# Eleven of layer 1's weight tiles split during layer 0's output product, and the parts of layer 1's weights kept in DRAM and reloaded by GpSimd's queue

## The chip, the core and the metric

The kernel runs on one core of a Trainium2 chip. A core has TensorE (PE, with its weight loads PEld), VectorE (DVE), ScalarE (ACT), GpSimd (POOL) and SyncE (SP), which share an on-chip memory; DMAs bring data from DRAM and back. Each engine works through its own list of instructions in order; a DMA is issued from the list of SP, ACT or POOL and stands in that engine's DMA queue. The metric is the time of one execution in microseconds on the device.

## The reference

Two layers on a residual stream of 1024 tokens by 1024 features, in float32. Layer 0 is a gated pooling mixer, layer 1 a gated sliding-window attention that reads one shared K/V. Cut to what matters:

```python
for l in range(2):
    shift, scale, gate = split(silu(c) @ ada_w[l] + ada_b[l], 3)
    if l == 0:
        h = rmsnorm(x, norm_g[0]) * (1 + scale) + shift
        u, z = split(h @ w_in, 2)
        p = pools(u) - u
        y = (group_matmul(p, w_group) * a_scale * silu(z)) @ w_out
    else:
        k, v = blocks((rmsnorm(x, kv_norm_g) * (1 + kvscale) + kvshift) @ w_kv)
        h = rmsnorm(x, norm_g[1]) * (1 + scale) + shift
        q, z = split(h @ b_w_in, 2)
        o = softmax_with_sinks(q * 64 ** -0.5 @ k + bias) @ v
        y = (o * silu(z)) @ b_w_out
    x = x + gate * y
return rmsnorm(x, final_g)
```

## The kernel before

Tokens lie along the free dimension, features on the 128 partitions. A float32 product is made of three matmuls: every operand is split into a rounded high part (ACT casts it) and the rest (DVE or POOL subtracts the high part), and high·high, high·low and low·high are added up in PSUM. A weight tile is 128 x 1024, 512 KB. `load_w` (line 133) fetches one on SP's queue into one of two `raw` buffers and splits it with `split_w` (line 119) into one of two pairs `wh`, `wl`.

The stages, in time: the pooling mixer's projections and pools (up to 424 us of the span); layer 0's output product (424 to 565); its last pieces, woven with the first norm of layer 1 (565 to 609); layer 1.

**Layer 0's output product** (lines 835 to 864) runs over `order`, 16 steps (n, half): output feature block n, half of the inner dimension. A step is 48 matmuls for n below `LATE` = 5 (both halves of the tokens, `q`), 24 after that. When the second half of an n is done, DVE adds it to `x` (`residual`), ACT squares and DVE sums the squares. The weights of step i+1 are fetched and split ahead of step i. `gather` brings back the gate products that the mixer kept in DRAM, `again_x` reloads `x`. Beside them `ada_step` (line 249) does the rest of the modulation: one of 48 tiles of `ada_rest` is loaded by SP into one of three `tmp` buffers, and DVE makes the dot product with `silu(c)` (`ada_dot`, line 239 in the profile). 18 of the 48 are done in the mixer, 30 here, with the table `ADA` of 16 numbers, one for each step. Here PE's order is written; the other engines' is left to the scheduler.

**Layer 1** (lines 1338 to 1376) runs over `specs`, for the first half of the tokens (q = 0) and then the second (q = 1): for each of four pairs of head rows two query tiles and two gate tiles of `wb` (`project`), between them the two tiles of `wkv` (`keys`, `values`), and output tiles of `wbo` (`project_out`, `out_quarter`). So most tiles are loaded and split twice, once for each half of the tokens. `load_w` for the next tile is called ahead of each product. `load_last` (line 1218) does the four `wbo` tiles of the second part with the subtraction on POOL. Beside the products the attention of block after block is woven in: `attend` has DVE and ACT make the scores and the softmax into `pt` (lines 1107 to 1119), PE transposes them (L1125), ACT and DVE split the result (`cur`, L1128 and L1129), POOL masks it (`prev`, `cur`, L1134 and L1137), PE multiplies with V (L1148). POOL also copies a column into each `pt` (L1093) and makes the low parts of modulated tiles (L167). PE's order is written here too, by a clock of estimated costs; the other engines' is the scheduler's.

## Time and profile before

| | us |
|---|---|
| median of three runs | 986.33 (985.83 to 986.64) |
| the profiled execution | 984.87 |
| its span, first to last instruction | 982.6 |
| PE busy in the span | 961.9 |
| the last chain, 962.6 to 982.6: statistics, POOL's multiplications (6.33), output | 20 |

In a window row the columns are: stretch, its length, then busy time (number of instructions) of PE, PEld, DVE, ACT and POOL, granted clock, share of the DMA engines and GB/s. In a row of a group: line, engine, operation, output and inputs, shapes, number, then busy time, mean ns of one, and idle time ahead of them with what ended it. A row of waits has the total, the number and the longest. A timeline row has start, duration, engine, line. A row of a DMA queue has packets, MB and the share of 16 engines; a row of DMA issues has the number, the size and the median time from issue to landing.

### The profile page before, as it was taken

The page shows a single profiled execution, that of the slowest core. Times are in us where ns is not written, and L with a number is a line of the kernel's source. Part 1 is how long each engine was busy: PE and PEld are TensorE (multiplying, and loading weights), DVE is VectorE, ACT ScalarE, POOL GpSimd, SP SyncE. Part 2 cuts the span into 40 slices and gives each one's busy share as a digit, 9 for nine tenths or more (in the row PEclk, how much of TensorE's full clock was granted, in tenths as well). Part 3 has the DMA queues.
Part 4 walks back from the last instruction along what each step waited for, and adds up shares of the span by engine and source line. Part 5 has one row for each costly group of instructions (what it writes and reads, how often), then busy time and mean ns, then how long its engine had stood idle before and what let it go on. Part 6 is the DMA issues. An engine that isn't in the chain of part 4 may idle for free.

```text
span 982.6 us, 12696 instructions
## 1 busy us (share of the span) xinstructions
PE 961.9 (98%) x4538; PEld 801.2 (82%) x4538; DVE 775.7 (79%) x1411; ACT 458.1 (47%) x902; POOL 145.0 (15%) x173
## 2 busy tenths in 40 slices
PE   8999999999999999999999999999999999999996
PEld 6788888888888887888888888877888888887786
DVE  5897978677978699676782278599899878889985
ACT  6534434333433244551111145486677546566544
POOL 2100000000000000000000000052324313335723
PEclk9999999999999999999999999999999999999998
DMA  9453622264225411779861223222211221223222
GB/s 331 183 174 114 192 103 65 78 201 150 65 85 194 150 64 57 262 267 327 305 216 65 86 64 130 86 65 69 82 66 64 87 86 65 64 88 106 86 87 86
DMA packets 40625, 125.67 MB, mean 128 GB/s; under 512 B 4465, under 2 KB 6641, under 8 KB 40434
## 3 DMA queue, kind: packets, MB, share of 16 engines
q1 hardware_dynamic: 40416, 123.82, 37.6%
q10 hardware_dynamic: 146, 1.05, 0.3%
q8 instruction: 35, 0.57, 0.2%
q14 instruction: 28, 0.23, 0.1%
HBM read 111.22 MB, written 13.63 MB: 127 GB/s over the span
## 4 chain that ended last, share of the span: by engine, by line
PE 78%; DVE 16%; issue 2%; ACT 2%; POOL 1%; DMA 0%; POOLq 0%; DVEq 0%; SPq 0%; ACTq 0%
PE ps_d L214 14%; PE ps_S L214 9%; PE ps_d L636 9%; PE ps_d L203 6%; PE ps_d L204 6%; PE ps_d L205 6%; PE ps_S L636 4%; PE ps_o L214 4%; PE ps_tp L214 3%; DVE wl L123 2%; PE ps_d L374 2%; PE ps_o L636 2%; PE ps_tp L636 2%; DVE tmp L542 2%; PE ps_tp L1125 1%
## 5 line engine op out<-in xcount | busy, mean ns | idle before, releaser
L121 ACT CAST wh<-raw 128x1024 fp32r<-128x1024 f32 x73 | 76.5, 1048 | 101.4 <-PE ps_d L214 78.5
L123 DVE TENSOR_TENSOR wl<-raw,wh 128x1024 fp32r<-128x1024 f32 x73 | 94.2, 1290 | 26.7 <-ACT wh L121 22.8
L203 PE MATMUL ps_d<-hm,wh 128*128 128x512 f32 x288 | 113.8, 395 | 0.0
L205 PE MATMUL ps_d<-hm,wl 128*128 128x512 f32 x288 | 112.4, 390 | 0.3 <-DVE wl L123 0.3
L204 PE MATMUL ps_d<-hm,wh 128*128 128x512 f32 x288 | 112.4, 390 | 0.0
L239 DVE CUSTOM_DVE_ANT_0 tmp<-tmp,cact,pk 128x1024 f32<-128x1024 f32 x48 | 60.7, 1282 | 33.2 <-DMA tmp<-ada_rest 32.9
L214 PE MATMUL ps_d<-gh,wh 128*128 128x512 f32 x224 | 82.0, 389 | 0.0
L214 PE MATMUL ps_S<-gh,wh 128*128 128x512 f32 x192 | 64.5, 390 | 0.0
L205 PEld LDWEIGHTS ps_d<-hm,wl 128*128 128x128 f32 x288 | 54.1, 188 | 12.6 <-DVE wl L123 1.1
L636 PE MATMUL ps_d<-hs,ws 128*128 128x512 f32 x264 | 63.4, 389 | 0.0
L1115 ACT ACTIVATE pt<-pt,nm 128x129 f32<-128x129 f32 x128 | 50.2, 394 | 26.8 <-DVE nm L1111 24.6
L203 PEld LDWEIGHTS ps_d<-hm,wh 128*128 128x128 f32 x288 | 54.1, 188 | 10.2
L204 PEld LDWEIGHTS ps_d<-hm,wh 128*128 128x128 f32 x288 | 54.2, 188 | 10.0
L636 PEld LDWEIGHTS ps_d<-hs,ws 128*128 128x128 f32 x264 | 49.5, 188 | 10.3
L542 DVE TENSOR_TENSOR tmp<-tmp 128x1039 f32<-128x1039 f32 (+3 forms) x40 | 49.4, 1235 | 6.8 <-ACT tmp L672 5.7
L612 ACT CAST ws<-tw 128x512 fp32r<-128x512 f32 x44 | 26.8, 621 | 53.9 <-PE ps_tp L214 15.1
L636 PE MATMUL ps_d<-ha,ws 128*128 128x512 f32 x216 | 51.9, 389 | 0.0
L534 POOL MEMSET tmp<- 128x16 f32 x16 | 1.7, 111 | 331.4 <-DVE tmp L542 115.9
L214 PEld LDWEIGHTS ps_d<-gh,wh 128*128 128x128 f32 x224 | 42.1, 188 | 8.7
L636 PEld LDWEIGHTS ps_d<-ha,ws 128*128 128x128 f32 x216 | 40.5, 188 | 8.4
L147 POOL TENSOR_TENSOR rs<-v,mhalf 128x4 f32<-128x4 f32 (+1 forms) x7 | 8.2, 1164 | 241.6 <-DVE v L145 241.6
L214 PE MATMUL ps_d<-gh,wl 128*128 128x512 f32 x112 | 43.6, 389 | 0.0
(294 smaller groups left out, 2492.0 us busy)
## 6 DMA issues: line engine op xcount, KB each, us to landing
tmp<-ada_rest SPq DMA_DIRECT2D x48, 512.0 KB, 4.7
raw<-wb SPq DMA_DIRECT2D x32, 512.0 KB, 3.3
raw<-wa SPq DMA_DIRECT2D x28, 512.0 KB, 3.7
raw<-wao SPq DMA_DIRECT2D x20, 512.0 KB, 4.1
ad<-ada_first SPq DMA_DIRECT2D x16, 512.0 KB, 5.0
x<-xT SPq DMA_DIRECT2D x32, 256.0 KB, 5.9
raw<-wbo SPq DMA_DIRECT2D x16, 512.0 KB, 3.3
kept_g<-tmp SPq DMA_DIRECT2D x14, 512.0 KB, 2.9
```

What stands on the lines that cost most here:

```text
L121: nc.scalar.copy(out=wh, in_=raw)
L123: nc.vector.tensor_sub(out=wl, in0=raw, in1=wh.bitcast(F32))
L203: mm(ps, lh, acts(k, 0), start=k == 0, stop=False)
L204: mm(ps, lh, acts(k, 1), start=False, stop=False)
L205: mm(ps, ll, acts(k, 0), start=False, stop=k == n - 1)
L214: mm(p, lhs, acts(k, hl, q), start=start and k == 0 and s == 0, stop=stop and k == n - 1 and s == 2)
L239: nc.vector.tensor_tensor_reduce(out=raw, in0=raw, in1=ca, scale=0.5, scalar=pk[:, bcol:bcol + 1], op0=ALU.mult, op1=ALU.add, accum_out=ad ...
L374: mm(psu[i, q], w0[k // 2][:, k % 2, w, i * P:(i + 1) * P], block(k, q)[hl], start=k == 0 and s == 0, stop=k == KT - 1 and s == 2)
L542: nc.vector.tensor_add(out=nx[:, 2 * s - 1:], in0=cur[:, 2 * s - 1:], in1=cur[:, s - 1:PAD + T - s])
L612: nc.scalar.copy(out=ws[i][:, 0, :], in_=src)
L636: mm(ps, lhs, acts(k, hl), start=start and k == 0 and s == 0, stop=k == 3 and s == 2, skip_group_check=True)
L1115: nc.scalar.activation(pt[:, i, :P + 1], pt[:, i, :P + 1], AF.Exp, bias=nm[:, i:i + 1], scale=-1.0, accum_out=den[:, i:i + 1])
```

## The change

`ADA` becomes six numbers for the first six steps (24 dots, loaded by SP as before). From step 6 on, the order of all five engines is written: the weights of step i+2 are fetched and those of step i+1 split, and a list `JOBS` of 6 dots (A) and 11 splits of `wb` tiles (S) is worked off, each with its load asked three jobs ahead on POOL's queue. The high part of such a tile goes to one of two `stage` slots, the low part replaces the tile in its `tmp` buffer; both are stored in DRAM by POOL's queue (`keep`). Layer 1 then takes the parts of a tile from DRAM where they are kept (`load_any`, two tiles ahead, three pairs of buffers by `pair_tiles`), on POOL's queue. A tile that isn't kept is loaded by SP, split, and its parts are stored by SP for the second half of the tokens; the parts of `wkv` and of the first query tile, split at the end of layer 0, are stored too. `load_last` goes: its four tiles are loaded by SP and split by ACT and DVE. In the tail two output products of the second half of the tokens come ahead of the four of the first half.

```diff
-ADA = (0, 0, 0, 2, 4, 4, 4, 4, 4, 4, 1, 1, 1, 1, 0, 0)
+ADA = (0, 0, 2, 6, 8, 8)
+BESIDE = 6
+JOBS = ("AAS", "AAS", "SSA", "SSA", "S", "S", "S", "S", "S", "")
...
+    def keep(key, hi, lo, queue=nc.sync):
+        kept_w[key] = [kp.tile([P, 1024], F32, name="kw") for _ in range(2)]
+        for dst, src in zip(kept_w[key], (hi, lo)):
+            queue.dma_start(dst, src.bitcast(F32))
+
+    def pair_tiles():
+        tags = (("raw", "raw"), ("wh", "wl"), ("wh", "wl"))[turns[0] % 3]
+        turns[0] += 1
+        return [wp.tile([P, 1024], F32R, tag=t, name="w2") for t in tags]
...
+            staged = [1, 8, 9, 2, 3, 10, 11, 4, 5, 12, 13]
+            def ask():
+                if not jobs:
+                    return
+                raw = tmp()[:, :1024]
+                kind = jobs.pop(0)
+                if kind == "A":
+                    i = rest_at[0]
+                    nc.gpsimd.dma_start(raw, ada_rest[i])
+                    rest_at[0] += 1
+                    asked.append(lambda: ada_dot(raw, cact, *rest_cols[i]))
+                else:
+                    i = staged.pop(0)
+                    nc.gpsimd.dma_start(raw, wb[i])
+                    asked.append(lambda: stage_split(i, raw))
+            def stage_split(i, raw):
+                hi = stage_hi[i % 2].rearrange("p a c -> p (a c)")
+                nc.scalar.copy(out=hi, in_=raw)
+                lo = raw.bitcast(F32R)
+                nc.vector.tensor_sub(out=lo, in0=raw, in1=hi.bitcast(F32))
+                keep(("b", i), hi, lo, nc.gpsimd)
...
+        with tc.manual_schedule(engines={ET.PE, ET.Activation, ET.DVE, ET.Pool, ET.SP}):
+            stage_hi = [slot("stage") for _ in range(2)]
+            raw = fetch(wao[order[BESIDE + 1]])
+            jobs, asked = list("".join(JOBS)), []
+            for _ in range(3):
+                ask()
+            for i in range(BESIDE, len(order)):
+                if i + 1 < len(order):
+                    ws[order[i + 1]] = split_w(*raw)
+                if i + 2 < len(order):
+                    raw = fetch(wao[order[i + 2]])
+                if i < KT:
+                    again_x(i)
+                for _ in JOBS[i - BESIDE]:
+                    asked.pop(0)()
+                    ask()
+                out_half(i)
...
+            if key in again:
+                keep(again[key], *w)
...
-    def load_last():
-        raw = wp.tile([P, 1024], F32, tag="raw", name="raw")
-        nc.sync.dma_start(raw, wbo[1, len(last_w)])
-        w = hp.tile([P, 2, T], F32R, tag="h", name="wo")
-        nc.scalar.copy(out=w[:, 0, :], in_=raw)
-        nc.gpsimd.tensor_sub(out=w[:, 1, :], in0=raw, in1=w[:, 0, :].bitcast(F32))
-        last_w.append((w[:, 0, :], w[:, 1, :]))
+    def load_any(key):
+        stays = key[0] == "o" and key[1] == 1
+        if stays:
+            t = hp.tile([P, 2, T], F32R, tag="h", name="wo")
+            w = t[:, 0, :], t[:, 1, :]
+            last_w.append(w)
+        else:
+            w = pair_tiles()
+        if key in kept_w:
+            for dst, src in zip(w, kept_w[key]):
+                nc.gpsimd.dma_start(dst, src)
+        else:
+            raw = bp.tile([P, 1024], F32, tag="raw1", name="raw1", bufs=2)
+            nc.sync.dma_start(raw, (wb if key[0] == "b" else wbo)[key[1:]])
+            nc.scalar.copy(out=w[0], in_=raw)
+            nc.vector.tensor_sub(out=w[1], in0=raw, in1=w[0].bitcast(F32))
+            if not stays:
+                keep(key, *w)
+        return w
...
-        *woven(project_out(0, 1) + project_out(1, 0)[:2], (0, 2, 4, 6)),
-        stats(0), project_out(1, 0)[2], finish(0, 4, FINISH[0]),
-        *project_out(1, 0)[3:],
+        *project_out(1, 0)[:2],
+        *project_out(0, 1),
+        project_out(1, 0)[2], stats(0), project_out(1, 0)[3], finish(0, 4, FINISH[0]),
+        project_out(1, 0)[4],
...
-        loaded = {srcs[0]: got["wq"]}
+        loaded = {srcs[0]: got["wq"], srcs[1]: load_any(specs[srcs[1]][0])}
...
-                nxt = srcs.index(i) + 1
+                nxt = srcs.index(i) + 2
                 if nxt < len(srcs):
-                    loaded[srcs[nxt]] = load_w(specs[srcs[nxt]][0])
+                    loaded[srcs[nxt]] = load_any(specs[srcs[nxt]][0])
```

What that does to the order, at three places. First DVE in layer 0's output product, around the end of step 9. Before, the last dot stands ahead of step 7's residuals, and from there on the rows are only weight splits (`wl`), two residuals (L686) and two sums of squares (L195) for each n:

```order
L239 ISA tmp_4271,adac_110<-tmp_4271,cact_119,pk_73 128x1024
L239 ISA adac_110 128x1
L686 SCALAR_TENSOR_TENSOR x_3425<-ps_tp_3856,adac_110,x_3425 128x512
L686 SCALAR_TENSOR_TENSOR x_3425<-ps_d_3857,adac_110,x_3425 128x512
L123 TENSOR_TENSOR wl_3998<-raw_3994,wh_3996 128x1024
L195 TENSOR_TENSOR sqh_3628<-sqh_3628,sq_3988 128x512
L195 TENSOR_TENSOR sqh_3630<-sqh_3630,sq_3991 128x512
L123 TENSOR_TENSOR wl_4066<-raw_4062,wh_4064 128x1024
L686 SCALAR_TENSOR_TENSOR x_3426<-ps_o_4000,adac_110,x_3426 128x512
L686 SCALAR_TENSOR_TENSOR x_3426<-ps_d_4001,adac_110,x_3426 128x512
L123 TENSOR_TENSOR wl_4140<-raw_4136,wh_4138 128x1024
```

The same place in the change, where `wl_4132` is the split for step 10 and `wl_4213` that for step 11 (L880 is `stage_split`, L258 the dot, L705 the residual):

```order
L258 ISA tmp_3997,adac_112<-tmp_3997,cact_121,pk_75 128x1024
L258 ISA adac_112 128x1
L128 TENSOR_TENSOR wl_4132<-raw_4059,wh_4130 128x1024
L880 TENSOR_TENSOR tmp_4067<-tmp_4067,stage_3896 128x1024
L880 TENSOR_TENSOR tmp_4075<-tmp_4075,stage_3895 128x1024
L258 ISA tmp_4078,adac_112<-tmp_4078,cact_121,pk_75 128x1024
L258 ISA adac_112 128x1
L705 SCALAR_TENSOR_TENSOR x_3428<-ps_o_4080,adac_112,x_3428 128x512
L705 SCALAR_TENSOR_TENSOR x_3428<-ps_d_4081,adac_112,x_3428 128x512
L214 TENSOR_TENSOR sqh_3636<-sqh_3636,sq_4205 128x512
L214 TENSOR_TENSOR sqh_3638<-sqh_3638,sq_4208 128x512
L128 TENSOR_TENSOR wl_4213<-raw_4134,wh_4211 128x1024
```

Two tile splits and a dot now stand between the weight split of step 10 and step 9's residuals, and the split for step 11 has moved behind the sums of squares. `tmp_4067` and `tmp_4075` are tiles 3 and 10 of `wb`, `tmp_4078` the last tile of `ada_rest`.

Second, POOL in the same stage. Before, its list has nothing there:

```order
L534 MEMSET tmp_2906 128x16
L534 MEMSET tmp_2925 128x16
L147 TENSOR_TENSOR rs_4367<-v_4365,mhalf_87 128x4
L1093 COPY pt_4811<-nsink_107 128x4
L1093 COPY pt_4889<-nsink_107 128x4
```

In the change 39 DMAs stand between the last memset and `rs`. Twelve of them, with `tmp_3925` tile 8, `tmp_3986` tile 9, `tmp_3989` tile 2, and `kw` the kept parts:

```order
L872 DMA tmp_3925<-wb 128x1024
L872 DMA tmp_3986<-wb 128x1024
L872 DMA tmp_3989<-wb 128x1024
L147 DMA kw_3993<-stage_3895 128x1024
L147 DMA kw_3994<-tmp_3925 128x1024
L867 DMA tmp_3997<-ada_rest 128x1024
L147 DMA kw_4063<-stage_3896 128x1024
L147 DMA kw_4064<-tmp_3986 128x1024
L872 DMA tmp_4067<-wb 128x1024
L147 DMA kw_4071<-stage_3895 128x1024
L147 DMA kw_4072<-tmp_3989 128x1024
L872 DMA tmp_4075<-wb 128x1024
```

The load of `tmp_3997` waits until the store from `tmp_3925` has landed, and the stores of tile 9 stand behind it; the load of `tmp_4067` waits for the dot on `tmp_3997`.

Third, POOL in layer 1, at the second half of the tokens. Before, a copy into `pt` and two masks for each block:

```order
L1134 AFFINE_SELECT prev_6403<-cur_6400 128x1024
L1137 AFFINE_SELECT cur_6400<-cur_6400 128x1024
L1093 COPY pt_6641<-nsink_107 128x4
L1134 AFFINE_SELECT prev_6534<-cur_6531 128x1024
L1137 AFFINE_SELECT cur_6531<-cur_6531 128x1024
L1093 COPY pt_6733<-nsink_107 128x4
```

In the change (L1165 is the copy, L1206 and L1209 the masks, `w2` a kept part on its way back):

```order
L1165 COPY pt_6744<-nsink_109 128x4
L1301 DMA w2_6675<-kw_4146 128x1024
L1206 AFFINE_SELECT prev_6641<-cur_6638 128x1024
L1301 DMA w2_6676<-kw_4147 128x1024
L1209 AFFINE_SELECT cur_6638<-cur_6638 128x1024
L1301 DMA w2_6709<-kw_4219 128x1024
L1301 DMA w2_6710<-kw_4220 128x1024
L1165 COPY pt_6834<-nsink_109 128x4
```

Each load waits until PE has left the buffer that it fills; here one stands ahead of both masks of a block and another between them. In all 66 such loads are in POOL's list.

More of the change, by code (lines that the diff above doesn't have):

```diff
@@ L66, in trunk @@
     pp = ctx.enter_context(tc.tile_pool(name="psum", bufs=1, space=PSUM))
+    kp = ctx.enter_context(tc.tile_pool(name="kept", bufs=1, space=bass.MemoryType.DRAM))
     BANKS = {"d": 4, "S": 2, "tp": 1, "o": 1}
@@ L1025, in keys @@
             return done(ps)
-        return wkv[0], lambda w: gemm_steps(w, 0, hk, KT, done)
+        return ("kv", 0), lambda w: gemm_steps(w, 0, hk, KT, done)
     vts = {}
@@ L1035, in values @@
             return done(ps)
-        return wkv[1], lambda w: gemm_steps(w, 0, hk, KT, done)
+        return ("kv", 1), lambda w: gemm_steps(w, 0, hk, KT, done)
     def values_split(q):
@@ L1177, in run @@
                 yield from gemm_steps(w, i * 512, acts, 4, done)
-        return wbo[part, n2], run
+        return ("o", part, n2), run
     def bare(f):
```

45 lines of the change are left out of this document (21 added, 24 removed).

## The prediction

> **What bounds the kernel now.** I read the page first, then the windows of each stage, then what PE waits for. Times count from the span's start.
>
> ```profile
> span 982.6 us, 12696 instructions
> PE 961.9 (98%) x4538; PEld 801.2 (82%) x4538; DVE 775.7 (79%) x1411; ACT 458.1 (47%) x902; POOL 145.0 (15%) x173
> 424.00:490.00 66.00, 66.00 (x293) 54.66 (x292) 46.12 (x70) 16.93 (x25) 0.00 (x0) 1.00 0.91 314
> 520.00:530.00 10.00, 10.00 (x46) 8.26 (x44) 1.23 (x1) 1.05 (x1) 0.00 (x0) 1.00 0.18 52
> 600.00:950.00 350.00, 342.72 (x1713) 286.85 (x1712) 304.83 (x712) 216.33 (x508) 125.19 (x118) 1.00 0.26 84
> 650.00:670.00 20.00, 16.75 (x85) 13.74 (x84) 19.68 (x45) 17.02 (x38) 13.28 (x12) 1.00 0.22 74
> PE ps_tp L1125 <- DVE pt L1119: 6.1, 5, 1.6
> PE ps_tp L154 <- POOL rs L147: 1.1, 1, 1.1
> ```
>
> PE sets the time, and its number of matmuls does not change. Only its idle time can move. In the window rows the number behind the length is PE's busy time: the two rows of layer 0's output product (424 to 565) have none idle, layer 1 from 600 to 950 has 350 − 342.72 = 7.3 us idle. 3.25 of these lie in 650 to 670, where DVE works 19.68 of 20 us. 6.1 us, in five waits, are waits of the softmax transposes for DVE's last multiplication. So the change can win at most about 7 us here, and can lose in layer 0 as well, where DMA is busy at a share of 0.91 until 490 and nearly idle later.
>
> **What layer 1 loses in work.**
>
> ```profile
> L123 DVE TENSOR_TENSOR wl<-raw,wh 128x1024 fp32r<-128x1024 f32 x45 | 60.0, 1334 | 12.2 <-ACT wh L121 9.9 <-PE ps_o L1149 1.7
> L121 ACT CAST wh<-raw 128x1024 fp32r<-128x1024 f32 x45 | 47.0, 1045 | 15.2 <-issue 7.6 <-PE ps_d L204 6.4 <-ACT qt L1062 0.9
> L1224 POOL TENSOR_TENSOR wo<-raw,wo 128x1024 fp32r<-128x1024 f32 x4 | 10.6, 2652 | 4.3 <-ACT wo L1223 4.2
> ```
>
> These rows are of 600 to 983. Layer 1 splits 49 tiles now: 45 casts on ACT with 45 subtractions on DVE, and 4 more with the subtraction on POOL. Afterwards 12 are left (4 of `wb`, 8 of `wbo`), all on ACT and DVE. DVE is relieved of 33 × 1.334 = 44 us, ACT of 37 × 1.045 = 39 us, POOL of 10.6 us. POOL gets 66 loads of parts. In 650 to 670 DVE had 45/350 × 20 = 2.6 splits, 3.4 us; with 16.3 of 20 us its queue no longer stays full, and the matmuls that waited for `pt` find it ready. I take all five waits away (6.1 us) and give back 0.4 for masks that come behind loads on POOL (below): **−5.7 us**. The bounds: −7.3 (everything idle) and −3 (half the waits stay, because ACT's part of the same chain becomes the late one).
>
> **Is a kept tile there in time?** The three pairs of buffers are used in turn. A pair comes free when PE ends the tile before the current one, and is needed two tiles on. A tile is 24 matmuls; at 342.72/1713 = 0.2 us each two tiles are 9.6 us, more with the attention between them.
>
> ```profile
> raw<-wao SPq DMA_DIRECT2D x7, 512.0 KB, 3.2
> q1 hardware_dynamic: 6346, 20.98, 87.5%
> tmp<-ada_rest SPq DMA_DIRECT2D x29, 512.0 KB, 4.9
> kept_g<-tmp SPq DMA_DIRECT2D x13, 512.0 KB, 2.9
> 438.78 0.33 SPq L130 DMA_DIRECT2D raw<-wao  x1
> ```
>
> A lone load of 512 KB lands after 3.2 us (first row, 530 to 600). In 440 to 510 20.98 MB went in 70 us at a share of 87.5%: 343 GB/s at a full share, 1.53 us for a tile. Two parts take 3.2 + 1.5 = 4.7 us, so 5 us of slack stay. POOL's queue is not in the trace: I take SP's 0.33 us per issue (last row) as the low end, and one DVE operation more per DMA, 1.3 us, as the high one.
>
> Masks and `pt` copies now stand between those loads on POOL. In before a mask ends 1.1 us (917.44 to 918.50) and 3.2 us (703.17 to 706.37) ahead of the matmul that reads it:
>
> ```profile
> 916.28 1.16 POOL L1137 TENSOR_SCALAR_AFFINE_SELECT cur<-cur 128x1024 fp32r<-128x1024 f32 x1
> 918.50 0.39 PE L1148 MATMUL ps_o<-cur,VS 128*128 128x512 f32 x1
> 702.08 1.09 POOL L1137 TENSOR_SCALAR_AFFINE_SELECT cur<-cur 128x1024 fp32r<-128x1024 f32 x1
> 706.37 0.39 PE L1148 MATMUL ps_o<-cur,VS 128*128 128x512 f32 x1
> ```
>
> One issue of 0.33 us fits in either gap, and an earlier `cur` from DVE adds room. So 0.4 us in all.
>
> **Layer 0's output product** has 16 steps: ten of 10.88 us, six of 5.44 (one half of the tokens). Step 9 ends at 532.46, steps 10 and 11 together are the row of 10.88, so step 11 starts at 538.1, step 8 at 510.9, step 6 at 489.1.
>
> ```profile
> L239 DVE CUSTOM_DVE_ANT_0 tmp<-tmp,cact,pk 128x1024 f32<-128x1024 f32 x22 | 27.8, 1283 | 19.0 <-DMA tmp<-ada_rest 18.7
> 532.46 0.75 DVE L686 SCALAR_TENSOR_TENSOR x<-ps_o,adac,x 128x512 f32<-128x512 f32 x1 [8.75 <-PE ps_o L214]
> 533.13 0.74 DVE L686 SCALAR_TENSOR_TENSOR x<-ps_d,adac,x 128x512 f32<-128x512 f32 x1
> 533.25 1.36 ACT L191 ACTIVATE sq<-x 128x512 f32<-128x512 f32 x2
> ...
> 532.65 10.88 PE ps_S L214 x48
> ```
>
> Before, 22 dots (first row) are done by 494. The change puts 24 ahead of step 6's written order, and takes two reloads of `x`, 3 us of DMA, from in front of them; I put the 24th at 494.8. Then come 6 dots and 11 splits (DVE 11 × 1.3, ACT 11 × 1.05 us, beside idle time: DVE works 1.23 of 10 us in 520 to 530), 17 loads and 22 stores on POOL. Three `tmp` buffers carry them, and a buffer comes free only when its store has landed. POOL waits for that in order, and all later stores and loads wait behind it. On DVE the last dot of step 9 stands ahead of step 4's two residuals, and these ahead of the split for step 11. That is the latest point. The chain, with 1.53 us per tile in POOL's own order, 1.7 more until a load has landed (3.2 − 1.5), 1.4 until a store has (2.9 − 1.5):
>
> - tile 1 asked at 495.0, split by 502.5 (DVE has residuals, a weight split, square sums and two dots first); four tiles stand in the queue from 500.1, so its store lands at 500.1 + 6.1 + 1.4 = 507.7
> - tile 8 asked then, split at 513.8; its store lands at 518.5, behind the loads of 9 and 2
> - the fifth ada tile is asked at 518.6, its dot ends at 523.4; tile 3 is asked, then tile 2's parts are stored by 529.7
> - the sixth ada tile is asked at 529.8, lands at 533.4; its dot follows tile 10's split, 535.5
> - two residuals 537.0, squares 538.3, cast 539.4, subtraction 540.3
>
> The low part is first read 0.45 us into the step, so PE waits 540.3 − 0.45 − 538.1 = 1.8: **+2 us**. The later steps have one tile each, and the same count leaves them 1 to 4 us. The bounds: 0, if the stores land as fast as alone, and +11 by the third rival.
>
> [...]
>
> **The sum.** −5.7 + 2 = −3.7. The profiled execution took 984.87 us (span 982.6 and 2.3 around it), so it would take 981.2; the median of the runs is 986.33, so **982.6 us**.
>
> **The rivals.**
>
> 1. The forecast, 978.5 to 984.3: chance 0.45.
> 2. DMA is full in layer 0, and gain and loss cancel. From 500 to 536 I count 9 loads and 8 stores on POOL, 4 weight tiles and 2 tiles of `x` on SP: 23 × 1.53 = 35 us in 36. For it: the rate above. Against: 1.8 us of the chain already have POOL's own queue in them. If three of SP's six tiles come between, +4.6: 986.33 − 5.7 + 6.6 = 987.2 us. Chance 0.22.
> 3. Slower: POOL's queue costs more per DMA than SP's. The chain has seven legs (four loads, three stores); each d more makes PE wait 7d in step 11. From d = 0.53 the gain is gone, from 0.8 it is slower by more than 0.2%. With d one DVE dot, 1.28: 986.33 − 3.7 + 9.0 = 991.6 us. For it: DVE works 46.12 of 66 us, and nothing in the trace shows POOL's queue free of it. Against: nothing shows it held either. Chance 0.17. [...]
> 4. The splits in layer 1 were hidden anyway: ACT's 17.02 of 20 us in 650 to 670 become the late part, 3 us are won, 3 to 4 lost: about 987. Chance 0.09.
> 5. POOL waits at a load for PE's buffer while a ready mask stands behind it. 28 blocks have masks; if half of them come two issues late (2 × 0.33, so 0.6 us), +8.4 in place of 0.4: 990.6 us. Chance 0.07.
>
> **How the numbers follow.** A measurement of this kernel can tell about 0.2%, 2 us. Rival 1 is nearly all faster (0.45, and 0.02 from the low sides of 2 and 4). Rivals 2 and 4 are mostly the same (0.26, the rest slower), 3 and 5 slower: 0.47, 0.26, 0.27. The range takes in −7.3 with no wait in layer 0 and the one wait for statistics gone too (last row of the first fence, 1.1): 977.9; and on the other side rival 3's price with the measurement's own spread: 978 to 992.5. The likeliest case's own range is 978.5 to 984.3.
>
> **What would show it.** Right: the waits for `pt` gone, DVE near 16 of 20 us from 650 to 670, 12 splits left; PE idle about 2 us near 538, with the weight cast or split named as what ended it; masks ending before their matmuls. Rival 2: DMA share near 1.0 from 500 to 540 and ada loads over 4.9 us. Rival 3: POOL's DMAs landing over 1 us later than 3.2 alone, PE idle 5 us or more there. Rival 5: waits of L1148's matmuls for POOL. What makes it wrong: the 24th dot later than 497, or ACT behind in step 8.

## The result, and the profile after

After the change the kernel takes 1003.9 us (median of six runs, 998.71 to 1004.67), before it 986.49 (six runs beside them): a ratio of 1.0168, 95% interval 1.0147 to 1.019. It is slower by 17 us, where 4 us of gain were forecast; the range of the forecast ended at 992.5.

The first fence has two lines of the page after, of the profiled execution of 1004.4 us. PE is busy 8.4 us longer with the same 4538 matmuls, and idle 32.4 us where it was idle 20.7.

```profile
span 1002.7 us, 12796 instructions
PE 970.3 (97%) x4538; PEld 808.6 (81%) x4538; DVE 743.5 (74%) x1389; ACT 434.0 (43%) x876; POOL 183.4 (18%) x274
```

Where the time went shows in two lengths that are read from every trace here: the output product of layer 0, from the start of its first matmul into `ps_d` to the start of its last (that is with its late pieces, but for one in `ps_S` that ends 11 us later), and the rest from there to the end. Stretches of the kernel before, then, in the second fence, of the one after, with three stretches of 10 us behind them (columns as in the windows above; the granted clock is the third number from the end):

```profile
423.90:588.30 164.40, 164.40 (x734) 136.37 (x733) 95.86 (x139) 39.95 (x55) 1.01 (x1) 1.00 0.57 191
588.30:982.60 394.30, 379.36 (x1963) 320.86 (x1961) 334.55 (x770) 237.91 (x551) 133.14 (x128) 0.99 0.25 83
```

```profile
425.40:607.50 182.10, 169.46 (x735) 138.68 (x734) 109.24 (x150) 50.54 (x66) 22.30 (x40) 0.96 0.76 267
607.50:1002.70 395.20, 380.49 (x1963) 323.82 (x1961) 288.77 (x737) 203.60 (x514) 149.60 (x190) 0.98 0.44 151
540.00:550.00 10.00, 1.22 (x2) 0.50 (x2) 6.42 (x8) 3.24 (x4) 3.79 (x7) 0.68 0.69 227
550.00:560.00 10.00, 9.98 (x36) 8.13 (x37) 4.25 (x4) 3.25 (x4) 1.63 (x3) 0.81 0.92 312
670.00:680.00 10.00, 7.30 (x33) 6.01 (x32) 9.86 (x17) 7.57 (x19) 7.01 (x8) 0.84 0.32 107
```

The output product takes 17.7 us more: 12.6 us idle (182.10 − 169.46), and 5.1 us (169.46 − 164.40) because the same matmuls take longer at a lower clock. The rest takes 0.9 us more, though DVE has 45.8 us and ACT 34.3 us less to do there: PE is idle in it for 14.7 us, where it was for 14.9, and busy 1.1 us longer. The remaining 1.5 us of the two spans lie ahead of 424, where kernels with the same code start this product anywhere from 422.8 to 426.8; so lengths are compared below, not spans.

What PE waited for after the change, from 490 on, and what POOL waited for from 490 to 600 (total, number, longest):

```profile
PE ps_S L233 <- ACT wh L126: 12.1, 2, 9.2
PE ps_tp L1197 <- DVE pt L1191: 5.8, 3, 2.7
PE ps_S L233 <- DVE wl L128: 0.5, 1, 0.5
```

```profile
POOL tmp L872 <- DMA kw<-tmp: 30.4, 4, 8.2
POOL tmp L867 <- DMA kw<-tmp: 11.0, 2, 7.3
```

The waits for `pt` in layer 1 are 5.8 us in three, as against 6.1 in five. New are the other two rows: PE waits twice for the cast of a weight tile, 9.16 us at step 11 and 2.91 at step 15, and once for a subtraction. And POOL stands 41.4 us for the store of a low part (`kw<-tmp`) to land, because a `tmp` buffer is not free before. The timeline of POOL shows its cycle in the chain that was forecast (bracket: idle time before, and what ended it), the last line, from PE's timeline, where it ends:

```profile
503.90 0.53 POOL L147 DMA_DIRECT2D kw<-tmp  x1 [0.15 <-issue]
512.60 1.79 POOL L872 DMA_DIRECT2D tmp<-wb  x3 [8.16 <-DMA kw<-tmp]
523.31 0.55 POOL L867 DMA_DIRECT2D tmp<-ada_rest  x1 [3.69 <-DMA kw<-tmp]
530.43 0.55 POOL L872 DMA_DIRECT2D tmp<-wb  x1 [5.43 <-DVE adac L258]
531.57 0.53 POOL L147 DMA_DIRECT2D kw<-tmp  x1
540.03 0.55 POOL L867 DMA_DIRECT2D tmp<-ada_rest  x1 [7.28 <-DMA kw<-tmp]
...
548.76 1.22 PE L233 MATMUL ps_S<-gh,wh 128*128 128x512 f32 x2 [9.16 <-ACT wh L126]
```

A store issued at 503.90 has landed when POOL goes on at 512.60, one issued at 531.57 when it goes on at 540.03. The dot of the tile asked for at 540.03 starts 4.5 us later, and on DVE and ACT the residuals, the squares and the cast for step 11 stand behind it. Not every store was so slow: one issued at 519.08 landed 3.84 us later. The stretches from issue to landing of the three differ in how busy the DMA engines were (the share is the last number but one):

```profile
503.90:512.20 8.30, 8.30 (x38) 6.90 (x37) 3.43 (x5) 0.00 (x0) 0.53 (x1) 1.00 0.88 326
519.08:522.92 3.84, 3.84 (x19) 3.18 (x18) 3.52 (x6) 3.46 (x5) 0.54 (x1) 1.00 0.65 260
531.57:539.63 8.06, 8.03 (x36) 6.32 (x34) 1.23 (x1) 1.05 (x1) 1.07 (x2) 1.00 0.90 310
```

The DMA issues of 490 to 600 (median us to landing):

```profile
kw<-stage POOLq DMA_DIRECT2D x11, 512.0 KB, 6.0
kw<-tmp POOLq DMA_DIRECT2D x11, 512.0 KB, 7.8
```

### The profile page after: what moved, and what is told of

It is laid out like the page before. It is cut to its first block, busy times and chain, and to the rows that moved or that the text cites. A ratio compares the mean times of both kernels' runs of the same rounds, so it can differ in the third digit from the quotient of the medians.

```text
span 1002.7 us, 12796 instructions
## 1 busy us (share of the span) xinstructions
PE 970.3 (97%) x4538; PEld 808.6 (81%) x4538; DVE 743.5 (74%) x1389; ACT 434.0 (43%) x876; POOL 183.4 (18%) x274
## 4 chain that ended last, share of the span: by engine, by line
PE 72%; DVE 10%; issue 7%; DMA 6%; POOL 2%; ACT 2%; POOLq 0%; SPq 0%; DVEq 0%; ACTq 0%
PE ps_d L655 9%; PE ps_d L222 9%; PE ps_d L223 9%; PE ps_d L224 9%; PE ps_d L233 7%; PE ps_S L233 5%; PE ps_S L655 4%; DMA tmp<-ada_rest 4%; PE ps_d L393 2%; PE ps_o L655 2%; PE ps_tp L233 2%; PE ps_tp L655 2%; DVE tmp L561 2%; PE ps_o L233 2%; PE ps_d L326 1%
## 5 line engine op out<-in xcount | busy, mean ns | idle before, releaser
L222 PE MATMUL ps_d<-hm,w 128*128 128x512 f32 x264 | 104.9, 397 | 0.0
L223 PE MATMUL ps_d<-hm,w 128*128 128x512 f32 x264 | 103.4, 392 | 0.0
L224 PE MATMUL ps_d<-hm,w 128*128 128x512 f32 x264 | 103.2, 391 | 0.0
L258 DVE CUSTOM_DVE_ANT_0 tmp<-tmp,cact,pk 128x1024 f32<-128x1024 f32 x48 | 60.7, 1283 | 34.3 <-DMA tmp<-ada_rest 34.3
L233 PE MATMUL ps_S<-gh,wh 128*128 128x512 f32 x192 | 67.6, 407 | 12.1 <-ACT wh L126 12.1
L224 PEld LDWEIGHTS ps_d<-hm,w 128*128 128x128 f32 x264 | 49.8, 189 | 10.8
L222 PEld LDWEIGHTS ps_d<-hm,w 128*128 128x128 f32 x264 | 49.9, 189 | 9.3
L223 PEld LDWEIGHTS ps_d<-hm,w 128*128 128x128 f32 x264 | 49.9, 189 | 9.1
L233 PEld LDWEIGHTS ps_S<-gh,wh 128*128 128x128 f32 x192 | 37.6, 198 | 20.7 <-ACT wh L126 12.9
L1301 POOL DMA_DIRECT2D w<-kw x66 | 35.8, 543 | 92.5 <-PE ps_d L224 56.1
L126 ACT CAST wh<-raw 128x1024 fp32r<-128x1024 f32 x28 | 29.4, 1049 | 42.3 <-PE ps_d L233 42.3
L1227 DVE SCALAR_TENSOR_TENSOR of<-ps_o,ol 64x256 f32<-64x256 f32 x64 | 26.6, 416 | 22.9 <-ACT ol L1223 22.4
```

The costliest lines, as they stand in the source:

```text
L126: nc.scalar.copy(out=wh, in_=raw)
L222: mm(ps, lh, acts(k, 0), start=k == 0, stop=False)
L223: mm(ps, lh, acts(k, 1), start=False, stop=False)
L224: mm(ps, ll, acts(k, 0), start=False, stop=k == n - 1)
L233: mm(p, lhs, acts(k, hl, q), start=start and k == 0 and s == 0, stop=stop and k == n - 1 and s == 2)
L258: nc.vector.tensor_tensor_reduce(out=raw, in0=raw, in1=ca, scale=0.5, scalar=pk[:, bcol:bcol + 1], op0=ALU.mult, op1=ALU.add, accum_out=ad ...
```

## The experiments

The theory after the result: in layer 0, stores on POOL's queue land late and hold the three buffers, so that POOL's cycle is longer than a step, and each wait of PE brings a lower clock behind it; in layer 1, two new waits eat the gain. The rivals: the DMA engines are full whatever queue issues; the written order on ACT and DVE is late by itself; the reloads on POOL's queue are what costs; the clock has another cause. 18 kernels were run. First the two lengths of each, from its trace, and its time beside the kernel before on the same chip:

| kernel | output product, us | rest, us | median, before beside it | ratio (95%) |
|---|---|---|---|---|
| before | 164.4 | 394.3 | 986.49 | |
| after | 182.1 | 395.2 | 1003.9, 986.49 | 1.0168 (1.0147–1.0190) |
| e1_stores_sp | 174.0 | 394.5 | 993.84, 984.4 | 1.0091 (1.0064–1.0118) |
| e2_no_stage | 164.4 | 400.0 | 990.48, 984.4 | 1.0056 (1.0034–1.0079) |
| e3_kept_sp | 187.6 | 395.4 | 1004.23, 984.4 | 1.0183 (1.0156–1.0210) |
| e4_stall | 178.7 | 394.6 | 999.02, 984.4 | 1.0143 (1.0122–1.0165) |
| e5_no_store | 164.3 | 401.1 | 993.49, 985.13 | one run |
| e6_stalls | 172.1 | 394.1 | 994.07, 985.13 | one run |
| e7_raw3 | 182.9 | 389.8 | 999.92, 985.13 | 1.0164 (1.0136–1.0192) |
| e8_low_dve | 183.8 | 392.8 | 1004.18, 985.13 | 1.0186 (1.0168–1.0205) |
| e9_six_sp | 164.4 | 396.9 | 989.04, 985.26 | 1.0032 (1.0021–1.0043) |
| e10_eleven_sp | 172.5 | 388.0 | 987.18, 985.26 | 1.0018 (1.0005–1.0031) |
| e11_before_low | 164.4 | 403.1 | 995.53, 985.26 | 1.0104 (1.0087–1.0120) |
| e12_six_pool | 164.4 | 398.5 | 990.56, 985.26 | 1.0052 (1.0036–1.0067) |
| e13_spread_sp | 173.7 | 390.2 | 988.52, 985.88 | 1.0024 (1.0009–1.0039) |
| e14_spread_pool | 188.6 | 390.1 | 1006.29, 985.88 | 1.0205 (1.0184–1.0225) |
| e15_spread_sp_low | 174.4 | 388.9 | 985.66, 985.88 | 1.0002 (0.9987–1.0016) |
| e16_nine_sp | 164.4 | 389.3 | 982.57, 986.26 | 0.9965 (0.9953–0.9978) |
| e17_nine_sp_low | 165.1 | 394.1 | 986.87, 986.26 | 1.0003 (0.9992–1.0014) |
| e18_nine_pool | 174.1 | 389.7 | 989.96, 986.26 | 1.0039 (1.0024–1.0054) |

After, e3, e7 and e8 have the same code in layer 0's output product, and took 182.1 to 187.6 us there: a length that hangs on when stores land varies by some 5 us. Each length comes from one traced execution. In e1, e2, e3, e4, e13 and e15 that was the longest on record, in e7, e9 and e16 the shortest; in e13 and e15 the median is 2.8 and 5.3 us below it, so that their output products stand near the upper end.

### Are the stores the cause in layer 0?

e1 gives the stores to SP's queue, e5 leaves them out:

```diff
-                keep(("b", i), hi, lo, nc.gpsimd)
+                keep(("b", i), hi, lo)            # e1: nc.sync
+                pass                              # e5
```

> The changed kernel with one edit: the 22 stores of split parts in layer 0's output product are issued by SP's queue, the 17 loads stay on POOL's. Theory A (POOL's queue lands stores late, 7.8 us from issue in the changed kernel's trace against 2.9 for SP's stores in the trace of before, and three buffers wait for that in order): the cycle of POOL falls from 8 to 9 us towards 5 to 6, the 9.2 us wait at step 11 and the 2.9 at step 15 shrink to under 2 us together, the clock does not fall near 550, and the time falls by 12 to 17 us to 987 to 992. Rival B (DMA as a whole is full there, whatever queue issues): stores still take about 7 us, PE idle near 548 stays over 6 us, 1000 to 1005. Rival C (the written order on ACT and DVE, not a queue): the waits stay as well, with POOL idle at the asks.

> The changed kernel with the 22 stores of layer 0's output product left out; the 11 tiles are loaded and split there in the same written order all the same, and layer 1 splits them again at their first use. Layer 0's output product (first to last matmul) took 164.4 us before, 182.1 after, 174.0 with the stores on SP's queue. Theory A2 (the stores are the cause: their landing holds the three buffers, and their 11.5 MB fill the DMA): waits for weight casts under 1 us, 164 to 166 us. Rival C (the written order on ACT and DVE, with a load's 4.7 us, is enough to be late): a wait of 3 us or more stays at step 11, 170 us or more. Layer 1 as without the staged tiles, some 400 us from there to the end.

Without the stores nothing is lost, 164.3 us (one execution), with the same loads, splits and order: so the stores, not the order of the work on ACT and DVE, make it late (rival C falls). On SP's queue 9.6 of the 17.7 us stay, more than theory A had: PE still waits 5.5 us for casts, where it expected under 2, and the time, 993.84, lies between theory A's and rival B's. The waits of PE in e1, then its windows:

```profile
PE ps_S L233 <- ACT wh L126: 5.5, 2, 5.1
```

```profile
540.00:550.00 10.00, 4.83 (x13) 3.12 (x12) 6.92 (x9) 2.84 (x4) 1.62 (x3) 0.66 0.97 354
560.00:570.00 10.00, 9.92 (x44) 8.18 (x44) 4.96 (x6) 2.74 (x3) 0.54 (x1) 1.00 1.02 396
```

Here rival B has its part: the DMA share is 0.97 to 1.02 (third column from the end is the clock, the last two are share and GB/s). In the kernel after it was 0.69 from 540 to 550, where PE stood for 8.8 us, and 0.88 and 0.90 behind the two slow stores. So there are two limits: with the stores in POOL's list the DMA engines are not kept busy throughout, and once SP's queue has them, the amount of data is the limit.

### How many tiles, and in which order?

```diff
-JOBS = ("AAS", "AAS", "SSA", "SSA", "S", "S", "S", "S", "S", "")
+JOBS = ("AA", "AAS", "AS", "AS", "S", "", "S", "", "S", "")           # six: e9, e12
+JOBS = ("AAS", "AAS", "AS", "AS", "S", "S", "S", "S", "S", "SS")     # eleven, spread: e13, e14, e15
+JOBS = ("AAS", "AAS", "AS", "AS", "S", "S", "S", "S", "S", "")       # nine: e16, e17, e18
```

The list `staged` is cut to match. All eight have three `raw1` buffers (e7, below); e9, e13, e15, e16 and e17 store by SP's queue, e12, e14 and e18 by POOL's; e9, e12, e15 and e17 have the subtractions on DVE (e8, below). e10, further down, is e1 with both of these edits.

> The six-tile version with the stores on POOL's queue, as in the changed kernel. Theory A (a store of POOL's queue lands late and holds one of three buffers even where the DMA engines have room): waits of PE for a weight cast of 1 to 6 us in the output product, 166 to 172 us. Theory L alone (only the amount of data counts): 164.4 to 166, as with SP's stores, and the stores land in 3 to 4 us on either queue.

> All eleven tiles, one in each of the steps 6 to 14 and two in step 15 rather than two in steps 8 and 9, stores on SP's queue, three raw buffers in layer 1. Theory L (the data asked for by step 11, eight tiles dense against five or six spread): the output product takes 164.4 to 167 us. Layer 1 takes 389.8 as with three buffers alone. Sum 2 to 5 us under before, ratio 0.995 to 0.998. Rival C2 (eleven tiles are too many in whatever order, the wait moves to steps 13 to 15): 169 to 174, ratio 1.001 to 1.005.

> The same spread order with the stores on POOL's queue, three raw buffers in layer 1. Theory A (POOL's cycle of ask, load, split, store and landing is 8 to 9 us a tile with stores of 6 to 8 us, against steps of 5.44 us from step 10 on): no wait at step 11, but waits in steps 12 to 15, 170 us or more for the output product. Theory L (only density counts): 164.4 to 167, as on SP's queue.

> The nine tiles with the stores on POOL's queue. Theory A (a cycle of 8 to 9 us on that queue against steps of 5.44): a wait of 5 us or more for a weight cast between 550 and 575, as with eleven (6.93 us at 569), output product 170 us or more. If only the number of tiles counts: 164.4 to 166.

Six tiles cost nothing on either queue (164.4), although POOL's stores still land in 6.3 and 6.5 us and theory A expected waits: a late store alone is harmless while steps leave room. Eleven are too many in either order: spread, the wait only moves to the end, to the sums of squares behind the last two tiles (5.2 us on SP's queue; 12.0 on POOL's, with 6.9 for a cast ahead of them). Nine tell the queues apart. Their DMA issues, e16 (SP) first, then e18 (POOL):

```profile
kw<-stage SPq DMA_DIRECT2D x9, 512.0 KB, 3.7
kw<-tmp SPq DMA_DIRECT2D x9, 512.0 KB, 6.2
```

```profile
kw<-stage POOLq DMA_DIRECT2D x9, 512.0 KB, 6.5
kw<-tmp POOLq DMA_DIRECT2D x9, 512.0 KB, 7.4
```

And what PE waited for in e18, which e16 lacks:

```profile
PE ps_S L233 <- ACT wh L126: 5.7, 1, 5.7
```

With nothing changed but the queue of 18 stores, 164.4 us become 174.1 (and the median of the runs 982.57 becomes 989.96). Two things differ: POOL's stores land later, and POOL's list has asks ahead of them that wait for an earlier store. The traces show both. From the end of a tile's split to the issue of its low part's store, e16 takes 0.03 us on average and e18 3.9, at most 11.5; from issue to landing, 5.7 and 7.0. So standing in POOL's list costs more than landing late, 3.9 as against 1.3 us for a tile. One tile of e18 was split by 544.77 and its low part stored at 556.30, behind two such asks:

```profile
543.54 1.23 DVE L880 TENSOR_TENSOR tmp<-tmp,stage 128x1024 fp32r<-128x1024 f32 x1 [1.53 <-ACT stage L878]
545.26 0.55 POOL L872 DMA_DIRECT2D tmp<-wb  x1 [8.26 <-DMA kw<-tmp]
...
555.10 0.55 POOL L872 DMA_DIRECT2D tmp<-wb  x1 [8.12 <-DMA kw<-tmp]
...
556.30 0.53 POOL L147 DMA_DIRECT2D kw<-tmp  x1
```

So the choice between POOL and SP changed this stage by 9.7 us, mostly because an ask that waits in POOL's list holds up the stores behind it: here the ask at 555.10 had waited 8.12 us, and the store came at 556.30.

### What does a wait of PE cost besides itself?

e4 and e6 are the kernel before, with the subtraction of a split repeated, so that PE waits and no DMA is added:

```diff
-                    ws[order[i + 1]] = half_w(*order[i + 1])
+                    rw, = fetch(wao[order[i + 1]])
+                    ws[order[i + 1]] = split_w(rw)
+                    for _ in range(10 if i + 1 == 11 else 0):          # e4
+                    for _ in range({11: 3, 15: 6}.get(i + 1, 0)):      # e6
+                        w = ws[order[i + 1]]
+                        nc.vector.tensor_sub(out=w[1], in0=rw, in1=w[0].bitcast(F32))
```

> The kernel before, with the subtraction of the split for step 11 of layer 0's output product done eleven times rather than once (the same values each time), about 13 us more of DVE, so that PE waits some 9 to 10 us at one place and nothing else changes. If an idle stretch of PE costs a lower granted clock behind it (theory A: 8.4 us of the changed kernel's loss are PE's busy time, not its idle time), the clock row behind the stall reads 0.8 to 0.9 for about 10 us and the time grows by the idle time and 2 to 5 us more: 998 to 1001. Rival E (the lower clock comes from something else in the changed kernel): clock 1.00 behind the stall, and the time grows by the idle time alone, 995 to 997.

> The kernel before, with the subtraction for step 11 done three more times and that for step 15 six more times: two waits of PE of some 2.5 and 5 to 6 us, 20 us apart. Before's own waits of 1.6 us left the clock at 1.00; one of 11.2 us made the next 20 us 5.6 us slower. If the lower clock follows every wait above some 2 us (theory F), PE is busy some 1 us longer behind the first and 2 to 4 us behind the second; if it needs a long wait (rival G), the first costs nothing but itself.

e4's wait and the stretches around it:

```profile
PE ps_S L214 <- DVE wl L846: 11.2, 1, 11.2
```

```profile
545.00:550.00 5.00, 0.00 (x0) 0.00 (x0) 4.86 (x5) 0.00 (x0) 0.00 (x0) 0.50 0.18 67
550.00:555.00 5.00, 3.02 (x7) 2.44 (x8) 1.89 (x2) 0.00 (x0) 0.00 (x0) 0.50 0.31 105
555.00:560.00 5.00, 5.00 (x17) 3.94 (x17) 0.00 (x0) 0.16 (x1) 0.00 (x0) 0.72 0.00 0
560.00:565.00 5.00, 5.00 (x23) 4.14 (x23) 2.58 (x3) 1.45 (x2) 0.00 (x0) 1.00 0.33 108
```

The output product takes 14.3 us longer for a wait of 11.2: the clock falls to 0.50 in the idle stretch and is full again some 6 us after PE starts, 3.1 us lost by that. (The 5.6 us in the expectation of e6 are from the whole spans, of which 2.2 lie ahead of the product and 0.3 behind it.) So the lower clock after the change follows from its waits (theory A), and rival E falls. e6's waits came out shorter than meant, 1.38 and 1.60 us, and left the clock at 1.00, so that they don't decide between theory F and rival G. One of 2.23 us, 7.5 us later, lowered it; yet in e11, further down, one of 2.94 us did not. The clock records in the traces show why. Wherever the clock changes from 420 to 940, the changes of one trace lie on a fixed grid of 3.41 us. Two steps of that grid in e6, with the wait of 2.23 us in the first, and three in e11, where the 2.94 us fall across the first two:

```profile
573.41:576.82 3.41, 1.18 (x9) 0.75 (x8) 1.45 (x2) 0.63 (x1) 0.00 (x0) 1.00 0.00 0
576.82:580.23 3.41, 3.41 (x11) 2.83 (x11) 0.16 (x1) 0.00 (x0) 1.01 (x1) 0.50 0.00 0
655.05:658.46 3.41, 1.97 (x9) 1.31 (x7) 3.35 (x10) 3.38 (x11) 0.00 (x0) 1.00 0.00 0
658.46:661.88 3.42, 1.92 (x15) 1.86 (x16) 3.33 (x8) 1.57 (x3) 0.19 (x1) 1.00 0.45 158
661.88:665.29 3.41, 3.41 (x17) 2.81 (x16) 3.41 (x14) 2.28 (x7) 2.37 (x2) 1.00 0.01 2
```

PE was idle for 2.23 us of e6's first step, and for 1.44 and 1.50 of e11's first two. In all 20 traces, from 420 to 940, 32 steps at full clock have PE idle for more than 1.8 us, and the step behind each of them is at 0.50; of some 2,900 with less, one (1.76 us, in e2) is followed by such a step. So in these traces it was the idle time within one step that counted, with the border at about 1.8 of its 3.41 us, and whether a wait of 2 to 3 us cost clock hung on where it fell on the grid: e6's 2.23 us in one step did, e11's 2.94 us across two did not.

### What became of layer 1's gain?

e2 takes the eleven tiles out of layer 0, so that layer 1 splits 23 rather than 12; e3 has SP issue the reloads:

```diff
+JOBS = ("AA", "AA", "A", "A", "", "", "", "", "", "")        # e2
-                nc.gpsimd.dma_start(dst, src)
+                nc.sync.dma_start(dst.bitcast(F32), src)     # e3
```

> The changed kernel without any of the 11 tiles split beside layer 0's output product: the six ada tiles stay on POOL's queue in the written order, and layer 1 splits these 11 tiles at their first use and keeps them (23 splits there rather than 12). Theory A (the loss is in layer 0, by buffers that wait for stores): no wait of PE for a weight cast between 490 and 565, clock 1.00 there, 985 to 990, that is at least 13 us under the changed kernel. Rival D (the loss is as much in layer 1, where POOL's reloads and SP's stores stand): 994 to 1002. If layer 1's own gain is real (7.3 us idle in before), the time is under before's 986.3 by 0 to 4.

> The changed kernel with the 66 reloads of kept parts in layer 1 issued by SP's queue rather than POOL's; layer 0 as in the changed kernel. Theory A (the loss is nearly all in layer 0): the 9.2 us wait at step 11 stays, and the time stays within 3 us of the changed kernel, 1001 to 1005. Rival D (POOL's reloads delay masks, statistics and pt in layer 1): the waits near 676 and 911 go and the time falls by 5 us or more, under 999.

In e2 layer 0 is as fast as before, but layer 1 takes 5.7 us more than before, with a wait of 3.87 us for `pt` at 664.55: between theory A's range and rival D's; the gain of 0 to 4 us that the expectation held possible did not come. e3's rest is 395.4 as against 395.2: the reloads on POOL's queue cost nothing that SP's doesn't, so rival D's reason falls. (Its layer 0 is unchanged code.)

Two waits are left to explain, at 676 and 911. e7 gives the raw tiles of layer 1 a third buffer, e8 has DVE make the low parts of the prepared tiles:

```diff
-            raw = bp.tile([P, 1024], F32, tag="raw1", name="raw1", bufs=2)
+            raw = bp.tile([P, 1024], F32, tag="raw1", name="raw1", bufs=3)     # e7
-                m.step(k)
+                m.step_h(k)                                                    # e8
+                m.step_l(k, nc.vector)
```

> The changed kernel with three buffers rather than two for the raw tiles that layer 1 still splits. In its trace the wait of 2.55 us at 911 has ACT's cast of a wbo tile before it, which waited 3.9 us for that tile's load, and the load had waited for a raw buffer. Theory H (the buffer): the third and fourth wbo tiles load earlier, the wait at 911 falls under 1 us, with the slow clock behind it, and the time falls by 2 to 4 us, to about 1000 to 1002. Rival I (the splits themselves stand ahead of pt in DVE's order): the wait stays over 2 us and the time the same.

> The changed kernel with the subtractions for the low parts of the second half's normalised tiles (16, 1.3 us each) moved from POOL to DVE. At 676 PE waits 2.70 us for pt behind three multiplications by rb that took 4.07 us on DVE rather than 3 times 0.68, while POOL subtracted. Theory J (DVE and POOL slow each other): the multiplications take 0.68 to 0.7 each, the wait at 676 falls under 1.3 us and layer 1 takes 2 to 4 us less (395.2 from the last matmul of the output product to the end in the changed kernel), 1000 to 1002. Rival K (too much work in one place, wherever it stands): the added 16 subtractions on DVE, 11 us or more, keep the wait over 2.5 us, 1003 to 1006.

An earlier cast of `wo`, which had waited 3.86 us for its load, in ACT's timeline, and the chain of work behind the wait at 911 in the kernel after, which ends at 910.98 (start, us, what):

```profile
904.43 1.05 ACT L1305 CAST wo<-raw 128x1024 fp32r<-128x1024 f32 x1 [3.86 <-DMA raw<-wbo]
```

```profile
907.20 0.94 ACT wo L1305
...
909.12 1.11 DVE wo L1306
910.23 0.61 DVE pt L1191
```

With the third buffer that wait is gone, and the rest is 389.8 us, 5.4 under the kernel after: 2.6 of idle time and 2.8 of PE's busy time. Part of the latter is chance: the wait near 676 stayed in e7 (2.69 us), but no lower clock followed it. By the time alone the two can't be told apart (1.0164 and 1.0168), since layer 0's scatter lies on top; e16, where layer 0 loses nothing, shows the gain in the time. At 676 it is the multiplications by `rb`; their durations from 655 to 680 (ns, least, median, most), in the kernel after and then in e8:

```profile
L196 DVE TENSOR_TENSOR xn<-x,rb x10: 679/684/1784, 658.7 to 675.9; 128x512 f32<-128x512 f32 x10
```

```profile
L196 DVE TENSOR_TENSOR xn<-x,rb x7: 680/683/692, 661.5 to 675.3; 128x512 f32<-128x512 f32 x7
```

Theory J holds there: none takes 1784 ns once POOL doesn't subtract beside it, the wait falls from 2.70 to 1.40 us, and the rest is 2.4 us shorter. The time (1.0186) does not show it; the output product of that trace is 1.7 us longer. In the kernel after, the three of the ten that began at 663.86, 670.39 and 672.07 took 1.76 to 1.78 us, each while POOL worked on subtractions (one of them alone takes 1.28, at 676.81), the other seven 0.68, 1.10 under the longest.

But as an edit it does not carry far:

> The kernel before with the one edit of the prepared tiles' subtractions on DVE rather than POOL. Its two waits of 1.60 and 1.65 us near 656 and 667 stand at the place of the changed kernel's wait at 676. Theory N (there DVE is full, 19.7 of 20 us, so that 16 more subtractions make it later): the waits grow to 4 us or more together, ratio 1.001 to 1.004. Theory J (the two engines slow each other, which goes): the waits fall under 1.5 us together, 0.997 to 0.999.

> A version meant to beat both: six tiles split beside layer 0's output product rather than eleven, at most one in a step, stores on SP's queue, three raw buffers in layer 1, the prepared tiles' subtractions on DVE. Without stores the output product took 164.3 us, as before; with eleven and SP's stores 174.0, the DMA share at 0.95 to 1.02 from 540 to 570. Theory L (eleven tiles' 16.5 MB don't fit beside the rest by then, six tiles' 9 MB do): 164.4 to 166. Layer 1: 389.8 with three buffers, 392.8 with DVE's subtractions alone (395.2 without either, 394.3 before), so 387 to 390 with both, and 0 to 3 more for five more splits. Sum 4 to 7 us under before: ratio 0.993 to 0.996. Rival M (what layer 1 wins goes into the stalls that more splits bring, 400 without staged tiles): 0.999 to 1.004.

> All eleven tiles, stores on SP's queue, three raw buffers in layer 1 and the prepared tiles' subtractions on DVE. If the two edits in layer 1 add up (each took one wait and the slow clock behind it away, 5.4 and 2.4 us): layer 1 takes 387 to 388, the output product 174 as with SP's stores alone, so 2 to 4 us over before, ratio 1.002 to 1.004. If they share a cause: 390 or more, 1.005 to 1.008.

> As the spread version on SP's queue, and the prepared tiles' subtractions on DVE. With twelve splits in layer 1 that edit took 1.8 us (389.8 to 388.0) and with eighteen it cost 7; here there are twelve: layer 1 388, 1 to 2 us under the version without it, ratio 0.993 to 0.997 if the output product is 164.4 to 167.

With twelve splits in layer 1 it wins 1 to 2 us (e10 and e15 against e7 and e13). In the kernel before, with 49 splits, it costs 8.8 us (theory N, and more than it had: waits of 2.94, 1.98 and 3.27 us), and with 14 or more it brings a wait of 3.56 us near 711 for DVE's `ps_S` (e9, e12, e17). DVE has no room there. e17, with the edit, has a rest 4.8 us longer than e16, without it; that e9 missed its aim for the same reason is likely, but six tiles without the edit were not run.

### A version that beats both

> Nine tiles in the spread order (one in each of the steps 6 to 14), stores on SP's queue, three raw buffers in layer 1, which splits 14. With eleven the DMA share was 1.01 from 550 to 570 and the one wait, 5.25 us, was for the squares behind the last two tiles, which are gone. Theory L: output product 164.4 to 166, layer 1 390 to 392: ratio 0.995 to 0.998. Rival M (two more splits in layer 1 bring new waits, 395 or more): 1.000 to 1.004.

> The same with the prepared tiles' subtractions on DVE: 1 to 2 us under the version without (as with eleven), if DVE has room for two more splits near the preparation; 5 us or more over it, as with six tiles, if not.

e16 (nine tiles in the spread order, stores by SP, three raw buffers, the subtractions left on POOL) takes 982.57 us, a ratio of 0.9965 to the kernel before (0.9953 to 0.9978). Its two lengths:

```profile
426.20:590.60 164.40, 164.40 (x735) 136.34 (x734) 107.15 (x148) 48.40 (x64) 9.37 (x16) 1.00 0.78 277
590.60:979.90 389.30, 377.76 (x1963) 321.07 (x1961) 291.57 (x739) 205.33 (x516) 148.55 (x186) 0.99 0.45 156
```

The work added to layer 0 costs nothing there, and the rest is 5.0 us shorter than before. With the edit, e17, nothing is left of that (1.0003).

## Why the prediction was wrong

- **What bounds the kernel.** PE's idle time was the right thing to count, but not all of it: the sum had no term for the clock. That omission is 5.1 us in the output product, and e4 shows it by itself (3.1 us behind one wait). The forecast read the clock as 1.00 in every row and took it as given, though its own price for a long wait needed it.
- **Layer 0, +2 us.** This is the term that failed: measured +17.7, 9.16 of it the wait at step 11 that was forecast as 1.8. The chain's order, its place and the engines were right, and of its seven legs (four loads, three stores) four came within 0.1 us of the forecast or under it. Three took longer: tile 1's store, from split to landed, 9.0 us for 5.2; the fifth ada tile, from ask to the end of its dot, 6.7 for 4.8; the storing of tile 2's parts, from that dot on, 10.0 for 6.4. That is 9.3 us too late, from 497 to 540. What was mis-sized is the price of a DMA among others: a store was put at 1.4 us more than its data, "(2.9 − 1.5)", from stores that SP issued in the mixer, where the DMA engines were at a share of 0.39 (the kernel before, 90 to 424), and the data was counted "in POOL's own order", without SP's. Behind the two late stores the share was 0.88 and 0.90, with one of SP's weight tiles under way each time. The later steps, to which the same count "leaves them 1 to 4 us", lost 3.4 us more, since POOL's asks come every 8 to 9.5 us there and a step is 5.44. The other 5.1 us are the clock.
- **Layer 1, −5.7 us.** Measured +0.9. The removed work was right (12 splits left, DVE down 45.8 us in that stretch), and no wait for a mask or for a reloaded tile came, as counted. Wrong was the step from work to waits: "with 16.3 of 20 us its queue no longer stays full". At the place of the first wait DVE works 9.86 of 10 us after the change too: what fills it is the preparation of the second half's tiles, whose multiplications took 1.76 to 1.78 us beside POOL's subtractions and 0.68 without. And a new wait of 2.55 us came at 911 from the four `wbo` tiles that now share two raw buffers. The gain itself was there to be had: with a third buffer and layer 0 out of the way it is 5.0 us (e16).
- **The rivals.** Rival 3 had the direction and the place right: later DMAs on POOL's queue, and a long wait at step 11. That its wait of 10.8 us (1.8 + 9.0) is close to the 9.16 measured is luck: it makes each of the seven legs later by 1.28 us, and four were not late, the other three by 1.9 to 3.8. Its 991.6 us was too low because it kept layer 1's gain, priced step 11 alone, and left the clock out: −5.7 against +0.9, 3.4 and 5.1 us. No run shows its term, a dot's time of DVE added to each DMA of POOL's queue; what the kernel after shows in its place is 0.54 us of POOL for an issue, and stores that landed 6.0 and 7.8 us after it (median, high and low parts). Rival 2, DMA full, is not what happened as a whole (a share of 0.77 from 500 to 540, and 0.69 from 540 to 550, where PE stood for 8.8 us), but SP's tiles between POOL's, which it names, have a part in the late legs, and it is the next limit, as e1 and e13 show. Rival 4 was near the outcome in layer 1, where the work taken away won nothing, but not for its reason: ACT works 7.57 of 10 us from 670 to 680, DVE 9.86. Rival 5's waits for masks did not occur in the kernel after; in e2, with more splits, they are 1.8 us.

## What to carry to other kernels

Work that is "hidden" beside a full engine must be priced by the cycle of its buffers, from ask to landed store on the queue that is really used and with the other DMAs of that stage, against the length of a step; with three buffers, eleven tiles were too many, and nine fitted once the stores stood in another list than the asks that wait for them. A wait of PE cost itself and, where it left PE idle for more than 1.8 us of a 3.41 us step of the clock, time at a clock of 0.50 behind it (3.1 us behind e4's wait of 11.2), while e6's waits of 1.38 and 1.60 us left the clock at 1.00: so here one long wait was worse than short ones that lie apart. Taking work from a busy engine wins only where that work stands in front of the late instruction.

## What the runs showed of the hardware

- Stores of 512 KB issued by POOL landed after 6.5 and 7.4 us (median, high and low parts, e18), those issued by SP after 3.7 and 6.2 (e16), though the DMA engines were busier in e16 (0.93 to 0.98 from 530 to 560, as against 0.64 to 0.84); with all eleven tiles the DMA engines were at 0.69 to 0.92 with POOL's stores and at 0.95 to 1.02 with SP's from 540 to 570.
- The DMA engines moved 396 GB/s at a share of 1.02 (e1, 560 to 570), more than the 343 that the forecast drew from the stretch before.
- An issue of a DMA kept POOL busy for 0.53 to 0.55 us (kernel after, 495 to 552); the forecast's low end was the 0.33 of one of SP's (before, 438.78).
- Where the granted clock changed from 420 to 940, it did so on a grid of 3.41 us in each trace. It fell to 0.50 behind every step at full clock in which PE was idle for more than 1.8 us (32 steps in 20 traces; in the kernel after the steps that begin at 540.19, 574.32, 673.31 and 908.83, with 3.41, 2.54, 2.70 and 2.15 us idle); in e4 and after the change it came back to 1.00 some 5 to 6 us after PE started again.
- Of DVE's ten multiplications by `rb` (128 x 512) from 655 to 680 in the kernel after, seven took 0.68 us and the three beside a subtraction of POOL 1.76 to 1.78; in e8, without the subtraction there, the longest of seven took 0.69.
